# A queue of its own for the substitution's steps in a planner that orders the engines' work

## The chip, the core and the metric

The kernel runs on one core of a Trainium2 chip. Five engines work beside each other, each with a queue that it runs in order: PE (TensorE, matmuls), DVE (VectorE), ACT (ScalarE), POOL (GpSimd) and SP (SyncE, which here issues all DMAs). The metric is the device time of one execution in microseconds (us); less is better.

## What is computed

One layer of a hybrid decoder for 2,048 new tokens and 8 short sequences of 4: a gated short convolution and an RWKV-7 branch on the same normalised input, merged by gates, projected, added to the input and normalised. Cut to its core:

```python
h = _rmsnorm(x, norm_g)
p = jnp.einsum('bsd,dn->bsn', h, w_in)                 # all projections: 1024 -> 10368 columns
u = cg * xin; conv = sum(conv_w[j] * u_ext[:, j:j + s] for j in range(CONV_W))
y_c = bg * conv * jax.nn.silu(zc)
xm = p_rwkv + (prev - p_rwkv) * mu_shift               # token shift: r, k, v, z and two small ones
def step(S, inp):                                      # per head, token after token
    sa = jnp.einsum('bhvk,bhk->bhv', S, -kk_t)
    S = S * d_t[:, :, None, :] + sa[..., None] * (kk_t * a_t)[:, :, None, :] + v_t[..., None] * k_t[:, :, None, :]
    return S, jnp.einsum('bhvk,bhk->bhv', S, r_t)
yn = group_norm(ys); y_r = (yn + bonus) * jax.nn.silu(zr)
m = jax.nn.sigmoid(gc) * (y_c @ w_out_c) + jax.nn.sigmoid(gr) * (y_r @ w_out_r)
out = rmsnorm(x + m @ w_o)
```

## The kernel before

**Tiling.** The 2,048 tokens are taken in four sets (`th`, 0 to 3) of 512 columns; the last also carries the 8 sequences. The 16 heads are taken in eight pairs (`p`). One round of the main loop is one pair of one set: 32 rounds. In each round PE runs a main stream of ten projection blocks or so (`Block`), each 24 matmuls of 128x128 by 512 columns (8 pieces of K, each as high x high, low x high, high x low, in fp32r). Matmuls of the other work are put between them.

**Blocks.** A block takes its weights with `take_w`. In the first set the weights come in as f32 (`wraw`); ACT writes the high part, DVE the low part (`whl<-wraw,whl`, in `w_lows`), and both go to DRAM, from where the later sets read them ready-made. A mixed block (k, r, v, z: `mixed_block`) begins with a copy on POOL of one column of what is carried over from the set before, `tmp<-carry`; when its matmuls are done ACT writes `tmp<-ip,vec`, DVE combines it into `kT`, `rT` or `vT` (`rT<-ip,omu,tmp`, which reads the column that POOL copied too), and POOL copies the last column back, `carry<-tmp`.

**Side work.** The RWKV recurrence of a pair is worked in chunks of 64 tokens, by generators that run beside the main stream: `rwkv_keys`, `rwkv_solve`, `rwkv_merge`, `rwkv_load`, `rwkv_chain`, `rwkv_out`. `rwkv_solve` inverts triangular blocks of 32 rows, all of a pair at once, by substitution on POOL, 31 rows from 31 down to 1, with two operations for each row, every one reading what the one before wrote:

```python
for j in range(31, 0, -1):
    c0 = j // 4
    G.tensor_tensor(out=tv, in0=Mi[:, j, 0:j]..., in1=X[:, c0:8, j:j + 1]..., op=ALU.mult)
    G.tensor_tensor(out=X[:, c0:8, 0:j], in0=X[:, c0:8, 0:j], in1=tv, op=ALU.add)
    yield W["inv"]
```

These 62 operations are "the steps" in what follows (`tt<-Mi,X` and `X<-X,tt` in the profile). When they are done DVE transposes X (`Mi<-X`), ACT copies it into place (`Xbd<-Mi`, four copies), DVE transposes two parts back (`Mc<-Xbd`), and PE multiplies them (`pt<-Mc,GM` and `pt<-Mc,Mo`, 16 small matmuls), all of it in `rwkv_merge` but the first. `rwkv_out` normalises the pair's rows before: sums on DVE, `nw` on DVE, a power on POOL (`mu<-nw,mhalf`, in `rsq_steps`), further DVE work; later two products of 512 columns on POOL. POOL also does one product of 512 columns for each convolution (`cv<-cv,tmp`) and small copies and fills for `pe`.

**What sets the order.** The program is written out by a planner. Every engine call goes through `Traced`, which has a cost for it in ns (`Traced.cost`), and `Clock.add` places it in planned time: not before its operands are ready (`_hits`), and in the first gap of its engine's list of busy stretches (`Clock.gap`). `Clock.busy` has one list each for DVE, ACT and POOL. Two operations of POOL of which one needs the other are placed at least 60 ns apart. `Clock.held` keeps POOL's operations and those of DVE that read two operands from SBUF off each other: a later placed one moves behind the other. An operation that has been placed is not moved again. At the end the operations of each of the three engines are sorted by planned start and chained in that order, except for kinds of work in `LOOSE`. `Clock.kind` is the kind of side work that is being written ("solve" for `rwkv_solve`, nothing for the main stream).

PE's queue is in the order in which the program is written. `Side.run` gives a generator its turn after each matmul of the main stream when its share of the round has come (`CUTS`: "solve" from 0.30 to 0.68 of a round in the first three sets) and when what it named in its last `yield` is ready in planned time, by `clock.ready` against `clock.t["PE"]`. The steps name nothing, so that those of a row are written as soon as the share allows, ahead of the planned time at which they run. The matmuls `pt<-Mc` are written when the plan has both `Mc<-Xbd` done.

Of the kernel before, what the change touches and what calls it, by code (L numbers as in the profile page):

```python
# [54 lines left out]
OVERLAP = {"DVE": (83, 13), "ACT": (60, 18)}  # L55


class Clock:
# [3 lines left out]
    def __init__(self):  # L62
        self.t = dict.fromkeys(("PE", "DVE", "ACT", "POOL", "SP"), 0.0)
        self.log, self.home = {}, {}
        self.mode = (128, 128)
        self.busy = {"DVE": [], "ACT": [], "POOL": []}
        self.touched = {}
        self.kind = None
        self.begun, self.planning = {}, False
        self.held = {"DVE": [], "POOL": []}  # L70
# [41 lines left out]
    def gap(self, eng, start, cost):  # L112


        b = self.busy[eng]
        if len(b) >= 200:
            start = max(start, b[0][1])
        i = len(b)
        while i and b[i - 1][1] > start:
            i -= 1  # L120
        for s, e in b[i:]:
            if s >= start + cost:
                break
            start = max(start, e)
        return start
# [5 lines left out]
    def ready(self, aps):  # L131
        return max([e[4] for ap in aps for e in self._hits(ap)], default=0.0)

    def add(self, eng, outs, ins, cost, lag=60.0, dual=False):
        start = max([self.t["PE"] - PAST if eng in self.busy else self.t[eng]] + [e[4] for ap in ins for e in self._hits(ap) if e[6] != eng] +
                    [e[4] - 26.0 if eng in OVERLAP else e[5] + 60.0 * (eng == "POOL") for ap in (*ins, *outs) for e in self._hits(ap) if e[6] == eng] +
                    [self.touched.get((eng, ap.tensor.name), 0.0) for ap in (*ins, *outs)] +
                    [e[5] + 60.0 * (e[7] != eng) for ap in outs for e in self._hits(ap)])
        took = cost
        if eng in OVERLAP:  # L140
            over, drain = OVERLAP[eng]
            p0 = self.boxes(outs[0])[0][0]
            took = cost - over if p0 == 0 else cost + over + 2 * drain
        if eng in self.busy:
            start = self.gap(eng, start, took)
        if eng == "POOL" or dual:
            for s, e in self.held["POOL" if eng == "DVE" else "DVE"]:
                if s <= start < e:
                    start = self.gap(eng, e, took)
                    break  # L150
            self.held[eng] = self.held[eng][-60:] + [(start, start + cost)]
        end = start + cost
        for ap in (*ins, *outs):
            self.touched[eng, ap.tensor.name] = start
        if eng in self.busy:
            b = self.busy[eng]
            i = len(b)
            while i and b[i - 1][0] > start:
                i -= 1
            b.insert(i, (start, start + took))  # L160
            del b[:-200]
        self.t[eng] = max(self.t[eng], end)
        for ap in ins:
            for e in self._hits(ap):
                if end > e[5]:
                    e[5], e[7] = end, eng
        for ap in outs:
            for p0, p1, f0, f1 in self.boxes(ap):
                old = self.log.setdefault(self.name(ap), [])
                old[:] = [e for e in old if not (p0 <= e[0] and e[1] <= p1 and f0 <= e[2] and e[3] <= f1)][-95:]  # L170
                old.append([p0, p1, f0, f1, end + lag, end, eng, eng])
        return start
# [77 lines left out]
class Traced:  # L250
# [23 lines left out]
    def cost(self, op, out, ins, k):  # L274
        n = out.free_size()
        if self.name == "PE":
            turned = op == "transpose"
            lhs, rhs = (ins[0], ins[1]) if turned else (k["lhsT"], k["rhs"])
            part = [next(x for x in (32, 64, 128) if v <= x) for v in (lhs.ap[0][1], lhs.free_size())]
            mode = tuple(part)  # L280
            if turned:
                t, late = max(0.85 * n, 30.0), 272.0
            elif rhs.dtype == F32R:
                mode, t, late = (P, P), 8 + 0.4375 * n, 175 + 0.43 * n
            elif mode == (P, P):
                t, late = max(1.667 * n + 3, 216.0), max(382.0 if n >= P else 328.0, 175 + 1.7 * n)
            elif mode == (32, 32):
                t, late = 30.5 * max(1.0, n / 32), 212.0
            elif mode[1] == 64:
                t, late = (59.6 if mode[0] == 64 else 55.4) * max(1.0, n / 64), 300.0  # L290
            elif mode == (64, P):
                t, late = (0.93 * max(n, 64) if n <= P else 0.93 * n), 250 + 1.7 * n
            else:
                t, late = 1.667 * max(n, 32), 300.0
            if mode != self.clock.mode:
                t, late = t + 165, late + 225
                self.clock.mode = mode
            return t, late - t + SLACK
        if self.name == "DVE":
            per = {"transpose": 1.12 if n <= 256 else 1.86, "tensor_tensor_scan": 2.1, "reciprocal": 6.1}.get(op, 1.05)  # L300
            if op == "tensor_reduce":
                n = ins[0].free_size()
            if op == "tensor_scalar" and ins[0].space != PSUM:
                per = 0.587
            one = op == "scalar_tensor_tensor" and isinstance(k["scalar"], bass.AP)
            return 145 + per * n + 58 * one
        if self.name == "ACT":
            strided = n > 64 and list(ins[0].ap)[-1][0] > 1
            return (155 if ins[0].space == PSUM else 190) + (1.9 if strided else 0.84) * n + 100 * max(0, len(ins) - 1) + 0.0
        if k.get("op") == ALU.pow:  # L310
            return 1650.0
        return 218 + 2.09 * n if op == "tensor_tensor" else 120 + 1.0 * n


class Queue:
# [26 lines left out]
def hybrid_kernel(tc, x_prompt, x_sample, state_conv, state_shift, state_rwkv, norm_g, w_in, conv_w,  # L342
# [1231 lines left out]
    def comb():  # L1574

        add, sub = ALU.add, ALU.subtract
        for w, src in (("c", w_out_c[0]), ("r", w_out_r[0]), ("o", w_o[0])):
            for j in range(4):
# [9 lines left out]
                if w == "o":  # L1588
                    for q in ("11", "12", "21", "22"):
                        yield from part_of(w, q, j, qr[q], 0.5)  # L1590
                    combined("11", "12", "11", sub)
                    yield from part_of(w, "t1", j, qr["11"], 0.5)
                    combined("12", "22", "12", sub)
                    yield from part_of(w, "t3", j, qr["12"], 0.5)
                    combined("22", "22", "11", sub)
                    yield from part_of(w, "t2", j, qr["22"], 0.5)
                    combined("21", "21", "22", sub)
                    yield from part_of(w, "t4", j, qr["21"], 0.5)
                else:
                    for q in ("11", "12", "21", "22") if w == "c" else ("11", "12", "22"):  # L1600
                        yield from part_of(w, q, j, qr[q])
                    combined("22", "21", "22", add)
                    yield from part_of(w, "s1", j, qr["22"])
                    combined("21", "11", "21", sub)
                    yield from part_of(w, "s3", j, qr["21"])
                    combined("22", "22", "11", sub)
                    yield from part_of(w, "s2", j, qr["22"])
                    combined("12", "12", "22", sub)
                    yield from part_of(w, "s4", j, qr["12"])
# [259 lines left out]
    def make(n, c, parts=(0, 1)):  # L1869
# [5 lines left out]
        src, js = Y if w != "o" else M, slice(2 * c, 2 * c + 2)  # L1875
        hi, lo = (ROOMS[n % 3][:, i, js, 0:wd] for i in range(2))
        add, sub = ALU.add, ALU.subtract

        def at(q):
# [251 lines left out]
```

## Time and profile before

| | us |
|---|---|
| median of 3 runs | 3110.27 (3109.02 to 3111.27) |
| the profiled execution | 3108.97 |
| its span, first to last instruction | 3107.1 |
| PE busy | 2999.2 |
| DVE busy | 1754.3 |
| ACT busy | 1341.9 |
| POOL busy | 894.9 |

A row of the page's groups has the line, the engine and the operation, what it writes and reads, how often, its busy time and the mean of one in ns, and the idle time of the engine before it with what ended it. The steps are two of POOL's rows and 311.2 + 313.1 = 624.3 us of its 894.9:

```profile
L260 POOL TENSOR_TENSOR tt<-Mi,X 128x60 f32<-128x60 f32 (+24 forms) x992 | 311.2, 314 | 492.3 <-DVE Mi L260 378.3
L260 POOL TENSOR_TENSOR X<-X,tt 128x60 f32<-128x60 f32 (+24 forms) x992 | 313.1, 316 | 77.5
```

All engine operations have line 260, that of the helper which records them, so groups are told apart by their tiles. Busy time of PE is from matmuls that are pipelined, with modelled ends; the granted clock is the share of full speed that the throttle left PE in a stretch.

### The profile page before, as it was taken

To read this page: it belongs to the slowest core of one execution; us is meant where nothing else is said; L and a number is where in the kernel's file an instruction comes from. 1 tells how busy PE (TensorE), PEld (TensorE's weight loads), DVE (VectorE), ACT (ScalarE), POOL (GpSimd) and SP (SyncE) were. 2 spreads that over 40 slices of the span, in tenths; PEclk is the share of its full clock that TensorE was granted. 3 is DMA by queue.
4 is the path that set the end of the run, shared out by engine and by line. 5 is a ranking of instruction groups with operands and counts; after the bars stand their busy time and mean duration, and the time that the engine had idled before them with its cause. 6 is when DMAs were issued, how large, how long until landed. Compare 5 with 4: busy or idle time off the path is not lost.

```text
span 3107.1 us, 56220 instructions
## 1 busy us (share of the span) xinstructions
PE 2999.2 (97%) x21418; PEld 2576.1 (83%) x21418; DVE 1754.3 (56%) x3634; ACT 1341.9 (43%) x2691; POOL 894.9 (29%) x2492
## 2 busy tenths in 40 slices
PE   7899898999999999999999999999999999999998
PEld 6677776788888888888888889998999898888996
DVE  5465555565555555655554445455555554486575
ACT  5454454454445445444444444444444442224223
POOL 2233333333333333333333333233333330000000
PEclk9999999999999999999999999999999999999999
DMA  8776676666766676666644445443444357988775
GB/s 270 245 226 218 213 251 208 210 228 212 240 223 233 233 239 235 224 230 235 234 175 160 160 146 178 142 136 124 142 142 143 126 168 233 348 324 298 279 258 191
DMA packets 293938, 659.16 MB, mean 212 GB/s; under 512 B 46394, under 2 KB 162227, under 8 KB 242982
## 3 DMA queue, kind: packets, MB, share of 16 engines
q1 hardware_dynamic: 293670, 655.58, 62.1%
q8 instruction: 169, 2.77, 0.3%
q14 instruction: 99, 0.81, 0.1%
HBM read 472.81 MB, written 182.69 MB: 211 GB/s over the span
## 4 chain that ended last, share of the span: by engine, by line
PE 64%; POOL 9%; issue 5%; DVE 5%; ACT 2%; DMA 1%; SPq 0%; POOLq 0%; DVEq 0%; ACTq 0%
PE ip L260 39%; PE acc L260 12%; PE pt L260 8%; POOL X L260 4%; POOL tt L260 4%; PE pb L260 3%; PE pa L260 1%; DVE tmp L260 1%; ACT Xbd L260 1%; DVE Mi L260 1%; DVE sq L260 0%; ACT tmp L260 0%; DMA Y<-yr 0%; DVE cv L260 0%; POOL cv L260 0%
## 5 line engine op out<-in xcount | busy, mean ns | idle before, releaser
L260 PE MATMUL ip<-XH,whl 128*128 128x512 f32 (+3 forms) x7088 | 1948.1, 355 | 54.2 <-DVE whl L260 35.9
L260 PEld LDWEIGHTS ip<-XH,whl 128*128 128x128 f32 x7088 | 1228.5, 190 | 198.5 <-DVE whl L260 40.7
L260 PE MATMUL ip<-XL,whl 128*128 128x512 f32 (+3 forms) x3544 | 1253.8, 354 | 1.2 <-POOL XL L260 1.2
L260 PEld LDWEIGHTS ip<-XL,whl 128*128 128x128 f32 x3544 | 675.5, 191 | 75.0 <-issue 8.6
L260 POOL TENSOR_TENSOR tt<-Mi,X 128x60 f32<-128x60 f32 (+24 forms) x992 | 311.2, 314 | 492.3 <-DVE Mi L260 378.3
L260 POOL TENSOR_TENSOR X<-X,tt 128x60 f32<-128x60 f32 (+24 forms) x992 | 313.1, 316 | 77.5
L260 DVE SCALAR_TENSOR_TENSOR S<-pb,pe,sp 64x64 f32<-64x64 f32 x512 | 143.9, 281 | 187.9 <-PE pb L260 180.0
L260 ACT ACTIVATE tmp<-ip,vec 128x512 f32<-128x512 f32 (+2 forms) x174 | 103.2, 593 | 277.0 <-PE ip L260 275.2
L260 ACT ACTIVATE sp<-S,pe 128x128 f32<-128x128 f32 x256 | 102.5, 400 | 207.4 <-DVE S L260 206.0
L260 DVE TENSOR_TENSOR UB<-pa,P 64x64 f32<-64x64 f32 x512 | 110.6, 216 | 129.2 <-PE pa L260 123.2
L260 ACT COPY SV<-pb 64x128 f32<-64x128 f32 x256 | 65.8, 257 | 234.7 <-PE pb L260 233.1
L260 POOL TENSOR_TENSOR f<-f,mhalf 128x1 f32<-128x1 f32 (+1 forms) x17 | 12.5, 742 | 459.9 <-DVE f L260 458.0
L260 DVE SCALAR_TENSOR_TENSOR rT<-ip,omu,tmp 128x256 f32<-128x256 f32 (+3 forms) x59 | 28.3, 509 | 188.4 <-POOL tmp L260 179.5
L260 POOL TENSOR_TENSOR cv<-cv,tmp 128x512 f32<-128x512 f32 (+1 forms) x32 | 48.2, 1507 | 279.6 <-DVE tmp L260 279.5
L260 POOL COPY pe<-tmp 128x8 f32<-128x8 f32 x40 | 11.1, 280 | 359.5 <-ACT tmp L260 346.8
L260 DVE TENSOR_TENSOR whl<-wraw,whl 128x1024 fp32r<-128x1024 f32 x81 | 101.6, 1257 | 21.4 <-ACT whl L260 20.5
L260 ACT COPY Xbd<-Mi 32x256 f32<-32x256 f32 x128 | 87.8, 686 | 59.3 <-DVE Mi L260 57.4
L260 PEld LDWEIGHTS pb<-UB,Xbd 128*128 128x128 f32 x512 | 86.7, 188 | 29.7 <-issue 6.7
L260 ACT ACTIVATE tmp<-ip 128x512 f32<-128x512 f32 (+2 forms) x126 | 62.9, 499 | 103.4 <-PE ip L260 99.1
L260 DVE TENSOR_TENSOR GM<-pt,mask_p 128x512 f32<-128x512 f32 x128 | 82.5, 686 | 44.2 <-PE pt L260 43.6
L260 PEld LDWEIGHTS pa<-S,AR 128*128 128x128 f32 x512 | 87.4, 188 | 23.7 <-DVE S L260 11.7
L260 PEld LDWEIGHTS pb<-SV,BKt 128*128 128x128 f32 x512 | 89.1, 188 | 21.0 <-ACT SV L260 7.1
(554 smaller groups left out, 4598.8 us busy)
## 6 DMA issues: line engine op xcount, KB each, us to landing
wraw<-in_w_in_dram SPq DMA_DIRECT2D x81, 512.0 KB
whl<-w_k SPq DMA_DIRECT2D x24, 1024.0 KB
whl<-w_r SPq DMA_DIRECT2D x24, 1024.0 KB
whl<-w_v SPq DMA_DIRECT2D x24, 1024.0 KB
whl<-w_z SPq DMA_DIRECT2D x24, 1024.0 KB
whl<-w_xin SPq DMA_DIRECT2D x24, 1024.0 KB
whl<-w_cg SPq DMA_DIRECT2D x24, 1024.0 KB
whl<-w_zc SPq DMA_DIRECT2D x24, 1024.0 KB
```

The costliest lines, as they stand in the source:

```text
L260: r = f(*a, **k)
```

## The change

A fourth list, "STEPS", joins the busy lists. An operation on POOL of kind "solve" looks for a gap in STEPS first and then in POOL's list, and is entered in STEPS alone. Any other operation on POOL looks for a gap in POOL's list, which holds no steps any more, and is entered there. So the steps keep out of the way of other operations that were placed before, and other operations are placed without regard to the steps; by the sorting at the end they come between them. The distance between two dependent operations of POOL becomes 75 ns for 60, and an element-wise operation of two tensors on POOL is costed at 190 + 2.05n ns for 218 + 2.09n, with n its elements in a partition. No operation is added, removed or changed. The diff:

```diff
-        self.busy = {"DVE": [], "ACT": [], "POOL": []}
+        self.busy = {"DVE": [], "ACT": [], "POOL": [], "STEPS": []}
...
-                    [e[4] - 26.0 if eng in OVERLAP else e[5] + 60.0 * (eng == "POOL") for ap in (*ins, *outs) for e in self._hits(ap) if e[6] == eng] +
+                    [e[4] - 26.0 if eng in OVERLAP else e[5] + 75.0 * (eng == "POOL") for ap in (*ins, *outs) for e in self._hits(ap) if e[6] == eng] +
...
+        queue = "STEPS" if eng == "POOL" and self.kind == "solve" else eng
         if eng in self.busy:
-            start = self.gap(eng, start, took)
+            start = self.gap(queue, start, took)
+            if queue == "STEPS":
+                start = self.gap(eng, start, took)
         if eng == "POOL" or dual:
             for s, e in self.held["POOL" if eng == "DVE" else "DVE"]:
                 if s <= start < e:
-                    start = self.gap(eng, e, took)
+                    start = self.gap(queue, e, took)
                     break
...
         if eng in self.busy:
-            b = self.busy[eng]
+            b = self.busy[queue]
...
-        return 218 + 2.09 * n if op == "tensor_tensor" else 120 + 1.0 * n
+        return 190 + 2.05 * n if op == "tensor_tensor" else 120 + 1.0 * n
```

## The prediction

> **What bounds the kernel now.** I read the busy shares of the page first, then the waits of PE, then those of DVE, and last the timeline around the longest waits.
>
> ```profile
> span 3107.1 us, 56220 instructions
> PE 2999.2 (97%) x21418; PEld 2576.1 (83%) x21418; DVE 1754.3 (56%) x3634; ACT 1341.9 (43%) x2691; POOL 894.9 (29%) x2492
> ```
>
> PE is the bound. No matmul is added or taken away, so the time can change only in PE's idle time and in its clock. PE's waits (who <- for whom: us in total, times, longest):
>
> ```profile
> PE ip L260 <- DVE whl L260: 35.9, 9, 11.3
> PE pt L260 <- DVE Mc L260: 12.9, 9, 4.3
> PE ip L260 <- DVE rT L260: 11.1, 4, 4.8
> PE ip L260 <- DVE vT L260: 4.7, 1, 4.7
> ```
>
> The reader is to see two kinds. In `whl`, `rT` and `vT`, 51.7 us together, PE waits for DVE in the projections. In `Mc`, 12.9 us, it waits for the result of the substitution, `rwkv_solve`. DVE's own waits name what holds DVE in the first kind:
>
> ```profile
> DVE rT L260 <- POOL tmp L260: 179.5, 27, 15.7
> ```
>
> 27 times DVE stands still because one small copy on POOL, `tmp<-carry` (the first column of a mixed block), is late. Why it is late stands in the timeline of one such place, DVE first, then POOL, then PE (start us, us, engine, line, operation, [idle before <- releaser]):
>
> ```profile
> 262.42 0.17 DVE L260 TENSOR_SCALAR nw<-mu__2816 128x8 f32<-128x8 f32 x1
> 274.04 0.75 DVE L260 SCALAR_TENSOR_TENSOR rT<-ip,omu,tmp 128x512 f32<-128x512 f32 x1 [11.45 <-POOL tmp L260]
> 274.71 0.43 DVE L260 STREAM_TRANSPOSE Mi<-X 128x256 f32<-128x256 f32 x1
> 275.07 1.18 DVE L260 TENSOR_TENSOR whl<-wraw,whl 128x1024 fp32r<-128x1024 f32 x1
> ```
>
> ```profile
> 273.56 0.21 POOL L260 TENSOR_TENSOR X<-X,tt 128x8 f32<-128x8 f32 x1
> 273.70 0.19 POOL L260 COPY carry<-tmp 128x1 f32<-128x1 f32 x1
> 273.82 0.18 POOL L260 COPY tmp<-carry 128x1 f32<-128x1 f32 x1
> 273.96 1.64 POOL L260 TENSOR_TENSOR mu__2816<-nw,mhalf 128x8 f32<-128x8 f32 x1
> ```
>
> ```profile
> 269.27 0.63 PE L260 MATMUL ip<-XH,whl 128*128 128x512 f32 x2
> 269.74 0.40 PE L260 MATMUL ip<-XL,whl 128*128 128x512 f32 x1
> 269.97 0.39 PE L260 MATMUL ip<-XH,whl 128*128 128x512 f32 x1
> 276.30 0.80 PE L260 MATMUL ip<-XH,whl 128*128 128x512 f32 x1 [5.94 <-DVE whl L260]
> ```
>
> The 62 steps of a substitution have filled POOL; the copies and the power `mu<-nw,mhalf` come right behind the last step, at 273.56, though the power's operand was there at 262.59. DVE sits at `rT`, the split of the next weights (`whl`) sits behind `rT`, and PE is idle for 5.94 us. In the plan of before the steps are 60 ns apart, no other operation fits between two, and so each takes its place after the last step placed so far.
>
> **What goes away.** Eight such places hold nearly all of the first kind. Here they are as stretches, each from PE's stop to the end of the slow clock behind it (the start and end of the stretch, us, then busy us of PE, PEld, DVE, ACT and POOL, the granted clock, DMA):
>
> ```profile
> 109.49:124.72 15.23, 3.94 (x10) 3.14 (x10) 3.68 (x4) 0.50 (x1) 7.88 (x33) 0.66 0.22 67
> 270.36:281.73 11.37, 5.43 (x14) 4.27 (x14) 6.02 (x12) 4.08 (x6) 5.51 (x18) 0.70 0.41 135
> 353.91:363.65 9.74, 2.95 (x7) 2.37 (x8) 5.02 (x10) 4.05 (x6) 6.18 (x21) 0.65 0.25 82
> 437.03:445.57 8.54, 2.98 (x8) 2.40 (x8) 4.00 (x5) 1.43 (x2) 4.95 (x18) 0.80 0.15 38
> 533.93:544.55 10.62, 3.81 (x9) 2.75 (x9) 6.12 (x13) 4.78 (x7) 4.92 (x18) 0.68 0.23 77
> 611.44:619.65 8.21, 4.28 (x12) 3.19 (x12) 6.19 (x13) 5.08 (x8) 4.33 (x13) 0.79 0.40 121
> 2135.67:2145.40 9.73, 4.96 (x21) 4.94 (x21) 1.66 (x6) 1.61 (x5) 7.59 (x26) 0.65 0.10 40
> 2459.67:2466.26 6.59, 3.26 (x13) 3.24 (x14) 1.60 (x5) 0.48 (x1) 5.34 (x20) 0.74 0.14 60
> sum 80.03, PE 31.61 PEld 26.31 DVE 34.30 ACT 22.01 POOL 46.70; mean PE 3.95 PEld 3.29 DVE 4.29 ACT 2.75 POOL 5.84
> ```
>
> In 80.03 us PE issues 94 matmuls. Undisturbed, three take 0.70 us (269.27 to 269.97 above), 0.233 each: 60 in the first six stretches make 14.0 us, and 34 in the last two, of about half that width, 4.0 us. So **80.0 - 18.0 = 62 us** go if no such stall is left. Its cover: with the copy between the steps, `rT` runs when its matmul is done, and the split is ready before PE asks.
>
> **What is moved, and its price on the chip.** The others now go between the steps. The copies cost nothing, as one that happened to fall there already shows:
>
> ```profile
> 916.55 0.32 POOL L260 TENSOR_TENSOR X<-X,tt 128x65 f32<-128x65 f32 x1
> 916.81 0.19 POOL L260 COPY tmp<-carry 128x1 f32<-128x1 f32 x1
> 916.95 0.30 POOL L260 TENSOR_TENSOR tt<-Mi,X 128x60 f32<-128x60 f32 x1
> ```
>
> Without it the step would start some 0.08 to 0.09 us after 916.87, which is where it starts. The copy lies in the pause in which a step waits for the one before. The power is too long for that pause: 1.64 - 0.09 = **1.55 us** by which the last step, and so X, comes later on the chip. The plan doesn't see this: all steps of the pair have been placed when the power is placed (in before it stands behind the last of them), and a placed step isn't moved. Queued behind the power on POOL are the remaining steps; for the last of them wait the transposition `Mi<-X` on DVE, the copies `Xbd<-Mi` on ACT, the transpositions `Mc<-Xbd` on DVE, and the matmuls `pt<-Mc` on PE. No DMA is issued from POOL here, and SP's queue keeps its order.
>
> **What the new costs do.** Steps are costed at 190 + 2.05n for 218 + 2.09n, and 75 ns apart for 60. The sizes n of a substitution's 62 operations, (8 - j//4)j twice for j = 31 to 1, add to 3,120. The plan's chain shrinks by 62 x (28 - 15) + 0.04 x 3,120 ns = **0.93 us**. PE's queue is written in the plan's order, with `pt<-Mc` where the plan holds X for finished. So PE comes to `pt<-Mc` 0.93 us earlier, while X comes 1.55 us later: 2.48 us against PE. That `rT` no longer stands before `Mi<-X` is known to the plan as well, so both sides gain the same from it.
>
> How much margin is there? Two pairs, one near each end: DVE's second `Mc`, and the first matmul of PE that waits for it or finds it ready.
>
> ```profile
> 929.62 0.43 DVE L260 STREAM_TRANSPOSE Mc<-Xbd 32x256 f32<-32x256 f32 x1 [0.16 <-ACT Xbd L260]
> 1670.58 0.44 DVE L260 STREAM_TRANSPOSE Mc<-Xbd 32x256 f32<-32x256 f32 x1 [0.56 <-ACT Xbd L260]
> ```
>
> ```profile
> 930.11 0.21 PE L260 MATMUL pt<-Mc,Mo 32*32 32x32 f32 x1 [0.38 <-DVE Mc L260]
> 1672.89 0.21 PE L260 MATMUL pt<-Mc,GM 32*32 32x32 f32 x1
> ```
>
> In the first the margin is -0.38 us (PE waits), in the second 1672.89 - 1671.02 = 1.87. I take the middle, 0.75, so a stall of 1.73 us in each of the 27 pairs in which DVE waited (27 in its row above): **46.7 us**. With a margin of 1.87 everywhere it would be 16, with -0.38 77. The other five pairs have no power in their steps and lose at most 0.93 each, **4.6 us**.
>
> Then the clock. Stretches with short stalls at `Mc`, same columns as above:
>
> ```profile
> 996.00:1006.00 10.00, 8.89 (x98) 6.76 (x96) 4.57 (x11) 7.70 (x15) 3.72 (x11) 1.00 0.77 270
> 1889.38:1896.23 6.85, 4.43 (x48) 4.24 (x48) 3.95 (x10) 6.24 (x12) 0.37 (x1) 0.75 0.39 146
> ```
>
> 1.11 us of idle time left the clock at 1.00; 6.85 - 4.43 = 2.42 us brought 0.75 over 6.85 us, 1.7 us lost. A stall of 1.73 lies between the two, so I count half of the 27: 13.5 x 1.7 = **23 us**, with none and all of them (46) as bounds.
>
> The Trainium skill, "TensorE: Matmul & The Clock Gate", section "Why this matters for your kernels", asks for no PE gaps above some 3 us, since one idle window brings back the half clock. By that rule stalls of 1.73 us would cost no clock; the stretch at 1889 speaks against it.
>
> **The sum**, from the profiled execution's 3108.97 us (its span and 1.9 us around it): 3108.97 - 62.0 + 46.7 + 4.6 + 23 = 3121.3. The median of the runs is 1.3 above the profiled one, so **3122 us**. The gain is on DVE's wait, and what is late next is X itself.
>
> **The rivals.**
>
> 1. *The margin holds.* If X isn't late on the chip by the power (because the plan puts `pt<-Mc` behind something else that is late enough), only 0.93 - 0.75 = 0.18 us x 27 = 5 us return: 3108.97 - 62 + 5, with the 1.3 some **3053 us**, faster. For it: 1.87 of margin at 1672.89. Against it: nine waits for `Mc` already, 12.9 us, with the power behind the steps. The point where it decides: with s the mean new stall, 27 x (s + 0.85) + 4.6 = 62 at s = 1.3 us. Below that the change gains.
> 2. *Short stalls leave the clock alone.* As the forecast, without the 23 us: **3099 us**. For it the row at 996, against it that at 1889.
> 3. *DVE slows the steps.* DVE, no longer held, does its work beside the steps:
>
> ```profile
> 260.44 1.35 DVE L260 TENSOR_TENSOR whl<-wraw,whl 128x1024 fp32r<-128x1024 f32 x1
> 260.78 1.17 POOL L260 TENSOR_TENSOR tt<-Mi,X 128x68 f32<-128x68 f32 x1
> ```
>
> A step of 68 elements took 1.17 us beside a split, against 0.32 for 65 elements above. One or two more of those per substitution, 0.85 each and unseen by the plan, make the stall about 2.7 us, 73 us for the 27, and all of them then halve the clock, 46 us: 3108.97 - 62 + 73 + 4.6 + 46, about **3171 us**. Against it: outside the first quarter few splits are left. The Trainium skill, "SBUF — State Buffer", section "Who interferes with whom", says that a DVE instruction with two SBUF inputs and a GpSimd one that reads SBUF exclude each other; the row agrees.
> 4. *It doesn't do what it says*: the others stay behind the steps, or PE's stalls only change place: **3110 us**. Against it: the power's operand is there 11 us before it runs.
>
> **How the numbers follow.** Forecast 0.35 (own range 3103 to 3148), rival 1 0.25, rival 2 0.17, rival 3 0.12, rival 4 0.11. The range, 3050 to 3152, leaves out about 0.08 below, for a full gain without any return, and 0.12 above. Within 0.2% (3104 to 3116.5; a measurement of this kernel tells about that much from no change) lie 0.06 of the forecast, 0.03 of rival 2 and 0.06 of rival 4: 0.15. Faster: rival 1, 0.13 of rival 2 and 0.02 of rival 4: 0.40. Slower: 0.29 of the forecast, 0.01 of rival 2, rival 3 and 0.03 of rival 4: 0.45.
>
> **What would show it.** DVE's wait for POOL `tmp` falls from 179.5 us to under 30; PE's for `whl`, `rT` and `vT` from 51.7 to under 8. The power stands among the steps, with X's last step 1 to 2 us further from the first. PE's wait for `Mc` rises from 12.9 to 40 to 80 us, with more short stretches at half clock. If the wait for `Mc` stays under 25 us, the step with the margin is wrong and the kernel is faster; if DVE still waits for POOL, the first step is.

## The result and the profile after

| | before | after |
|---|---|---|
| median of 12 runs, us | 3110.62 (3107.74 to 3114.31) | 3120.95 (3110.93 to 3131.42) |
| ratio, 95% interval | | 1.0032 (1.0019 to 1.0045) |
| profiled span, us | 3107.1 | 3123.8 |
| PE busy, us | 2999.2 | 3026.6 |
| span less PE busy, us | 107.9 | 97.2 |
| mean granted clock | 0.989 | 0.982 |

The change costs 0.3%. The profiled execution after took 3125.49 us, 4.5 us more than the median, so that its rows are those of one of the longer runs. Of the twelve runs of the last kernel in the table of experiments two took 8418 and 8569 us at full clock, why isn't known, and its figures leave them out. The last three rows hold the surprise: PE is idle for 10.7 us less than before, and the kernel is slower, because PE is busy for 27.4 us more with the same 21,418 matmuls. The page after:

```profile
span 3123.8 us, 56082 instructions
PE 3026.6 (97%) x21418; PEld 2604.2 (83%) x21418; DVE 1770.9 (57%) x3634; ACT 1341.2 (43%) x2691; POOL 905.6 (29%) x2492
```

Where PE is idle has changed altogether. The groups of PE in the kernel after, then the same groups before (xcount | busy, mean ns of one | idle time before them, and what ended it):

```profile
L263 PE MATMUL ip<-XH,whl 128*128 128x512 f32 (+3 forms) x7088 | 1961.9, 356 | 7.7 <-DVE whl L263 7.2 <-DVE tmp L263 0.2
L263 PE MATMUL pt<-Mc,GM 32*32 32x32 f32 x512 | 28.6, 202 | 28.6 <-DVE Mc L263 16.0 <-DVE u L263 6.0 <-DVE Yc L263 4.2
L263 PE MATMUL pt<-Mc,Mo 32*32 32x32 f32 x512 | 24.7, 203 | 18.4 <-DVE Mc L263 18.3
```

```profile
L260 PE MATMUL ip<-XH,whl 128*128 128x512 f32 (+3 forms) x7088 | 1948.1, 355 | 54.2 <-DVE whl L260 35.9 <-DVE rT L260 11.1 <-DVE vT L260 4.7
L260 PE MATMUL pt<-Mc,GM 32*32 32x32 f32 x512 | 24.5, 195 | 7.3 <-DVE Mc L260 7.3
L260 PE MATMUL pt<-Mc,Mo 32*32 32x32 f32 x512 | 22.7, 195 | 5.6 <-DVE Mc L260 5.6
```

Before the projections PE was idle for 54.2 us and is now for 7.7. Before `pt<-Mc` it was idle for 7.3 + 5.6 = 12.9 and is now for 28.6 + 18.4 = 47.0. Of these 47.0 us 34.2 are put down to `Mc`, and two stalls of 6.0 us together, put down to `u`, end 0.15 us behind the end of an `Mc`; most of the remaining 6.8 us ends with `Yc` or with an operation on ACT. DVE no longer waits for the copies, and waits for X instead:

```profile
DVE Mi L263 <- POOL X L263: 81.9, 26, 6.6
```

Before, that row read 19.3 us, and `rT` waited 179.5 for POOL's `tmp`, a row that is gone.

One pair shows the whole of it. POOL's timeline after (start us, us):

```profile
890.09 0.24 POOL L263 TENSOR_TENSOR tt<-Mi,X 128x31 f32<-128x31 f32 x1 [10.62 <-DVE Mi L263]
...
913.02 0.24 POOL L263 TENSOR_TENSOR X<-X,tt 128x28 f32<-128x28 f32 x1
913.23 1.65 POOL L263 TENSOR_TENSOR mu__9342<-nw,mhalf 128x8 f32<-128x8 f32 x1
914.84 0.23 POOL L263 TENSOR_TENSOR tt<-Mi,X 128x24 f32<-128x24 f32 x1
...
916.38 0.65 POOL L263 TENSOR_TENSOR X<-X,tt 128x8 f32<-128x8 f32 x1
```

The power stands between two steps: the next starts at 914.84, where 913.26 + 0.08, the usual pause, would be 913.34. That is 1.50 us. From the first step's start to the last one's end it is 917.03 - 890.09 = 26.94 us. The same pair before:

```profile
900.67 0.59 POOL L260 TENSOR_TENSOR tt<-Mi,X 128x31 f32<-128x31 f32 x1 [15.20 <-DVE Mi L260]
...
925.78 0.21 POOL L260 TENSOR_TENSOR X<-X,tt 128x8 f32<-128x8 f32 x1
```

925.99 - 900.67 = 25.32 us, 1.62 less. PE, after, stands still for that pair twice, for 0.77 us at 917.97 and for 1.10 before the second `Mc`:

```profile
917.34 0.63 PE L263 MATMUL ip<-XH,whl 128*128 128x512 f32 x2
918.74 0.24 PE L263 MATMUL pt<-Mc,GM 32*32 32x32 f32 x2 [0.77 <-DVE Mc L263]
```

And the clock falls to half behind it. Behind a stall of nearly the same size in another pair, the second row, it doesn't (start and end of the stretch, us, then busy us of PE, PEld, DVE, ACT and POOL, the granted clock, DMA):

```profile
917.97:930.21 12.24, 10.37 (x86) 8.15 (x85) 4.12 (x6) 7.21 (x14) 2.86 (x4) 0.58 0.51 175
1071.83:1083.83 12.00, 10.18 (x130) 8.17 (x130) 2.41 (x5) 8.29 (x17) 3.06 (x5) 1.00 0.61 187
```

Both stretches have 1.8 to 1.9 us of idle time. In the first PE gets 86 matmuls done in 12.2 us, in the second 130. The idle time is the small part of the cost in the first of these pairs.

### The profile page after: what moved, and what is told of

Same layout as the page of the kernel before. It is cut to its first block, busy times and chain, and to the rows that moved or that the text cites. A ratio compares the mean times of both kernels' runs of the same rounds, so it can differ in the third digit from the quotient of the medians.

```text
span 3123.8 us, 56082 instructions
## 1 busy us (share of the span) xinstructions
PE 3026.6 (97%) x21418; PEld 2604.2 (83%) x21418; DVE 1770.9 (57%) x3634; ACT 1341.2 (43%) x2691; POOL 905.6 (29%) x2492
## 4 chain that ended last, share of the span: by engine, by line
PE 57%; POOL 19%; issue 11%; DVE 8%; ACT 3%; DMA 2%; SPq 0%; POOLq 0%; DVEq 0%; ACTq 0%
PE ip L263 33%; PE acc L263 12%; POOL X L263 8%; POOL tt L263 8%; PE pt L263 8%; PE pb L263 2%; DVE tmp L263 2%; ACT Xbd L263 2%; PE pa L263 1%; DVE Mi L263 1%; POOL cv L263 1%; DVE whl L263 1%; ACT tmp L263 1%; DMA gc<-tmp 1%; DVE cv L263 1%
## 5 line engine op out<-in xcount | busy, mean ns | idle before, releaser
L263 PEld LDWEIGHTS ip<-XL,whl 128*128 128x128 f32 x3544 | 681.1, 192 | 71.7 <-issue 4.1
L263 POOL TENSOR_TENSOR tt<-Mi,X 128x60 f32<-128x60 f32 (+24 forms) x992 | 318.0, 321 | 487.2 <-DVE Mi L263 400.3
L263 POOL TENSOR_TENSOR X<-X,tt 128x60 f32<-128x60 f32 (+24 forms) x992 | 321.5, 324 | 71.4
L263 PE MATMUL pb<-UB,Xbd 128*128 128x128 f32 x512 | 103.3, 284 | 4.5 <-DVE UB L263 3.8
L263 PE MATMUL pa<-S,AR 128*128 128x128 f32 x512 | 101.4, 280 | 5.8 <-DVE S L263 5.7
```

The costliest lines, as they stand in the source:

```text
L263: r = f(*a, **k)
```

## The experiments

My theory: the gain is real (DVE is free, PE's stalls in the projections are gone) and is given back because PE's queue has `pt<-Mc` earlier than X is there, by the power among the steps and by a planned chain that has become 0.93 us shorter; short stalls then halve the clock. The rivals: DVE's work beside the steps slows them; or PE's place for `pt<-Mc` isn't what costs. In the table "idle at `Mc`" is PE's idle time before the matmuls `pt<-Mc`, and "at half clock" the time in which the trace's record of the clock shows half, without the last stretch behind the final matmuls; both, and the mean clock, are those of the profiled execution. Each ratio is to the kernel before, run on the same chip.

| kernel | median, us | ratio to before, 95% | idle at `Mc` | at half clock | mean clock |
|---|---|---|---|---|---|
| before | | 1 | 12.9 | 64.9 | 0.989 |
| after | 3120.95 | 1.0032 (1.0019 to 1.0045) | 47.0 | 109.2 | 0.982 |
| queue alone, old costs | 3108.21 | 0.9987 (0.9978 to 0.9997) | 33.8 | 85.3 | 0.985 |
| new costs alone, old queue | 3117.77 | 1.0018 (1.0009 to 1.0026) | 16.8 | 81.9 | 0.986 |
| after, power behind the steps | 3078.33 | 0.9893 (0.9878 to 0.9908) | 21.8 | 44.4 | 0.992 |
| after, steps planned 115 ns apart | 3108.72 | 0.9990 (0.9980 to 1.0000) | 37.6 | 88.7 | 0.985 |
| after, X counted 1.25 us later | 3094.91 | 0.9949 (0.9936 to 0.9963) | 32.9 | 71.7 | 0.988 |
| after, X counted 2.5 us later | 3068.14 | 0.9865 (0.9852 to 0.9877) | 18.0 | 44.4 | 0.992 |
| after, X counted 3.75 us later | 3068.33 | 0.9868 (0.9852 to 0.9885) | 8.0 | 34.1 | 0.993 |
| after, X counted 5.0 us later | 3067.72 | 0.9857 (0.9842 to 0.9872) | 6.8 | 30.7 | 0.994 |
| power behind, X counted 1.0 us later | 3083.41 | 0.9917 (0.9904 to 0.9929) | 13.0 | 51.2 | 0.991 |
| before, X counted 1.0 us later | 3106.82 | 0.9983 (0.9975 to 0.9992) | 2.9 | 78.5 | 0.986 |

**The two halves of the change, each alone.** The queue with the old costs:

```diff
-... e[5] + 75.0 * (eng == "POOL") ...
+... e[5] + 60.0 * (eng == "POOL") ...
-        return 190 + 2.05 * n if op == "tensor_tensor" else 120 + 1.0 * n
+        return 218 + 2.09 * n if op == "tensor_tensor" else 120 + 1.0 * n
```

> The queue of its own, with the old costs (218 + 2.09n, 60 ns). Theory (PE comes to pt<-Mc before X is there, partly by the power between the steps, partly by the plan's chain that shrank by 0.93 us): the plan's X is 0.93 us later than in the changed kernel, so PE's idle time before pt<-Mc falls from 47 us to about 20 to 30, half clock from 109 us to 60 to 85, time 3085 to 3105. DVE's wait for POOL tmp stays under 15 us. Rival (the steps are slowed by DVE's work beside them, by several us, or the gain was never there): 3115 to 3130, idle before pt<-Mc above 40 us.

And the new costs in the kernel before, the same lines the other way round:

> The new costs (190 + 2.05n, 75 ns) in the kernel before, one list for POOL. Theory: DVE's wait for POOL tmp stays near 180 to 200 us and the stalls of the first kind stay; PE comes 0.93 us earlier to pt<-Mc, its idle time there goes from 13 us to 20 to 35; time 3115 to 3135, slower than before. Rival (the shrunk chain is harmless, the return comes from the power alone): 3105 to 3115.

The queue alone is 0.13% faster than before, and the shrunk costs take it from there to 0.32% slower. By themselves, in the kernel before, they cost 0.18%. Both go the theory's way, and both less far than it said: the queue alone still has 33.8 us of idle time at `Mc` where 20 to 30 were expected, and its time, 3108.21, is above the range given; with the new costs alone the idle time is 16.8 us where 20 to 35 were expected. A planned chain that is 0.93 us longer doesn't make up for a power of 1.5 us.

**The power put behind the steps again.**

```diff
-        queue = "STEPS" if eng == "POOL" and self.kind == "solve" else eng
+        queue = "STEPS" if eng == "POOL" and (self.kind == "solve" or cost == 1650.0) else eng
```

> The changed kernel, but the power (cost 1650) is placed in the steps' list too, so behind the steps as before; the copies stay between them. Theory: X comes 1.55 us earlier on the chip than in the changed kernel, idle time before pt<-Mc from 47 to under 20 us, half clock under 70 us, DVE's wait for POOL tmp under 15 us: 3050 to 3085, faster than both. Rival (X is late because of DVE's work beside the steps, the power is nothing): idle before pt<-Mc stays above 35 us, 3110 to 3125.

3078.33 us, 1.1% faster than before and in the range given, and the stalls in the projections stay away; the idle time at `Mc`, 21.8 us, is just above the 20 expected. Its groups of PE:

```profile
L263 PE MATMUL ip<-XH,whl 128*128 128x512 f32 (+3 forms) x7088 | 1942.6, 354 | 6.1 <-DVE whl L263 5.4 <-ACT whl L263 0.4 <-DVE tmp L263 0.2
L263 PE MATMUL pt<-Mc,GM 32*32 32x32 f32 x512 | 25.8, 197 | 11.3 <-DVE Mc L263 6.9 <-DVE Yc L263 2.5 <-DVE u L263 1.4
L263 PE MATMUL pt<-Mc,Mo 32*32 32x32 f32 x512 | 23.1, 197 | 10.5 <-DVE Mc L263 10.5
```

So with the copies alone among the steps the gain stays, and with the power among them too, in the changed kernel's plan, it is given back. This run is no clean test of the rival that DVE's work beside the steps is what makes X late, since its steps, 628.0 us in all, are faster than the changed kernel's as well. How much longer the steps have become there shows in their two groups on POOL (x992 each: busy us, mean ns):

```profile
L263 POOL TENSOR_TENSOR tt<-Mi,X 128x60 f32<-128x60 f32 (+24 forms) x992 | 318.0, 321 | 487.2 <-DVE Mi L263 400.3
L263 POOL TENSOR_TENSOR X<-X,tt 128x60 f32<-128x60 f32 (+24 forms) x992 | 321.5, 324 | 71.4
```

318.0 + 321.5 = 639.5 us in all, against 624.3 in the kernel before: 15.2 us, or 0.5 us for each of the 32 substitutions. It is there, at a third of the power's price. Worked out from all 32 substitutions, the time from the first step to the end of the last grew by 2.14 us, from 24.42 to 26.56: 1.3 by the power, 0.5 by the slower steps, 0.4 by copies and products of 512 columns among the steps.

**The plan alone, first way: steps further apart.**

```diff
-... e[5] + 75.0 * (eng == "POOL") ...
+... e[5] + (115.0 if self.kind == "solve" else 75.0) * (eng == "POOL") ...
```

> The changed kernel, with the steps planned 115 ns apart for 75: the plan's X comes 62 x 40 ns = 2.48 us later, on the chip nothing is longer. Theory: PE comes to pt<-Mc when X is there; idle time before it from 47 us to under 10, half clock under 45 us, 3045 to 3070. Rival (the stalls at pt<-Mc are not a matter of where PE's queue has it; X's end itself holds the main stream by other ways): 3105 to 3125, the idle time moves to other matmuls.

3108.72 us: better than the changed kernel, far from what the theory said. The mean time from a substitution's first step to the end of its last is 27.79 us here. Where the plan stretches the steps, more of what comes later falls among them, and the chip, whose steps aren't stretched, has to run it there. So in this kernel:

```profile
601.88 0.23 POOL L263 TENSOR_TENSOR X<-X,tt 128x24 f32<-128x24 f32 x1
602.07 1.28 POOL L263 TENSOR_TENSOR tmp<-tmp,bv 128x512 f32<-128x512 f32 x1
603.31 0.21 POOL L263 TENSOR_TENSOR tt<-Mi,X 128x16 f32<-128x16 f32 x1
```

```profile
1436.25 0.18 POOL L263 COPY carry<-tmp 128x1 f32<-128x1 f32 x1 [0.58 <-ACT tmp L263]
```

A product of 512 columns has come between two steps (12 of `rwkv_out`'s products are among steps here, 4 in the changed kernel), and elsewhere POOL stands for 0.58 us at a copy whose operand isn't there yet, with steps behind it. The idle time before such operations among the steps is 0.76 us for each substitution, worked out from all 32, against 0.11 in the changed kernel. The margin in the plan was 2.48 us, and the chip took back 27.79 - 26.56 = 1.23. This edit was no clean test. What is left of the margin, 1.25 us, also brought less than the same 1.25 us in the next test; why is open.

**The plan alone, second way: only X's end.** Steps and others keep their places; the plan counts X as readable later.

```diff
-        took = cost
+        took, lag, self.late = cost, lag + self.late, 0.0
...
+            clock.late = 1250.0 if j == 1 else 0.0
             G.tensor_tensor(out=X[:, c0:8, 0:j], in0=X[:, c0:8, 0:j], in1=tv, op=ALU.add)
```

> The changed kernel; the plan counts X as finished 1.25 us after its last step, and nothing else differs (steps stay 75 ns apart in the plan, so others aren't moved among them). Theory (PE's place for pt<-Mc against X is what costs): idle time before pt<-Mc from 47 us to 15 to 25, half clock from 109 us to 50 to 75, 3070 to 3095. If a step's distance of 115 ns failed because X itself came later by it, this works where that didn't. Rival (PE's place isn't it): 3110 to 3125 and idle time of PE about as in the changed kernel, 97 us.

> The same with 2.5 us. Theory: idle time before pt<-Mc under 12 us, half clock under 50 us, 3050 to 3075. Rival: as in the run with 1.25 us, or slower, if what follows X now comes too late for the next round.

> As with 2.5 us, with 3.75. Each 1.25 us brought 26 to 27 us so far (3121, 3095, 3068), and 18 us of idle time before pt<-Mc are left at 2.5, most of it waits of 1.09 us for the second Mc. Theory: these go, idle before pt<-Mc under 9 us, half clock under 35 us, 3050 to 3062. Rival (at 2.5 us the margin covers X, and more only makes what follows late): 3064 to 3080, idle time in ip, pa and pb grows.

> As above, with 5.0 us: where the return ends. Theory: nothing is left to win at pt<-Mc, within 8 us of the run with 3.75. Rival: the rounds no longer hold the work, idle time before pa and pb rises over 15 us, slower than with 3.75 by 10 us and more.

3121, 3095, 3068, 3068, 3068 us: 26 and 27 us for the first two steps of 1.25, then nothing. No operation on the chip is shorter here, and POOL's order differs only where the rest of the plan moved with it. The times with 1.25 and 2.5 are in the ranges that were written down, though the idle time at `Mc` fell less than expected (32.9 us for 15 to 25, 18.0 for under 12). With 3.75 the idle time and the half clock are as expected, and the time is above its range, in that of the rival; with 5.0 it is within the 8 us expected. With 2.5 us the power is still among the steps, and the kernel is 1.35% faster than before. These are its two groups at `Mc` on PE and the steps on POOL:

```profile
L263 PE MATMUL pt<-Mc,GM 32*32 32x32 f32 x512 | 24.9, 196 | 6.6 <-DVE Mc L263 3.6 <-DVE u L263 3.0
L263 PE MATMUL pt<-Mc,Mo 32*32 32x32 f32 x512 | 22.9, 196 | 11.4 <-DVE Mc L263 11.3
L263 POOL TENSOR_TENSOR X<-X,tt 128x60 f32<-128x60 f32 (+24 forms) x992 | 324.1, 327 | 72.0
L263 POOL TENSOR_TENSOR tt<-Mi,X 128x60 f32<-128x60 f32 (+24 forms) x992 | 318.4, 321 | 487.5 <-DVE Mi L263 374.6 <-PE ip L263 23.9 <-DVE S L263 18.7
```

The steps take 324.1 + 318.4 = 642.5 us, no less than in the changed kernel, and the power is where it was: X is as late on the chip, and only what reads it has another place in the plan. The margin moves the place of DVE's `Mi<-X` as well as that of `pt<-Mc`; the runs don't part the two. Two of its pairs, with the same stall of 1.09 us for the second `Mc`:

```profile
895.85:903.14 7.29, 6.20 (x67) 4.82 (x69) 2.91 (x3) 5.37 (x10) 2.87 (x4) 0.77 0.65 223
971.59:978.88 7.29, 6.20 (x84) 4.94 (x83) 2.89 (x3) 6.12 (x12) 2.87 (x4) 1.00 0.68 226
```

7.29 - 6.20 is the same 1.09 us of idle time in both; in one the clock halves and 67 matmuls get done, in the other 84. With 3.75 us the idle time at `Mc` falls to 8 us, but PE waits longer elsewhere, 7.9 us for 4.0 for DVE's `Yc` before the transpositions of the pair before and 5.6 for 1.7 for `S` before `pa`. Its idle time as a whole falls by 4 us only, and its busy time not at all, though the half clock is 10 us less; why is open.

**Both remedies together, and the margin without the queue.**

> The power behind the steps, and X counted as finished 1.0 us after its last step. Theory: of the 21.8 us before pt<-Mc that were left with the power behind, under 10 remain; half clock under 40 us; 3050 to 3070, the fastest. Rival (what is left comes from elsewhere): 3073 to 3083 as with the power behind alone.

> The kernel before, with X counted as finished 1.0 us after its last step. It shows what a margin is worth without the new queue. Theory: the 13 us before pt<-Mc fall to under 6 with their share of the half clock, and the stalls of the first kind stay: 3093 to 3107. Rival (the margin, not the queue, is what the faster kernels live on): 3050 to 3085.

The first did not do what I expected. With the power behind the steps a margin of 1.0 us lowers the idle time at `Mc` from 21.8 to 13.0 and the kernel is slower, 3083 for 3078. Its trace has PE standing 5.6 us for `whl` and 3.6 and 3.8 us elsewhere in the first set, with DVE at `Mi<-X` for 4 to 5 us each time; why that set came out worse than without the margin stays open. In the kernel before, the margin takes the idle time at `Mc` from 12.9 to 2.9, as expected, and the time falls by 0.17%, at the upper end of the range given. The half clock did not fall with the idle time (78.5 us for 64.9), and the stalls before the projections remain, 56.8 us for 54.2. That settles the rival that the margin alone is what the faster kernels live on: it is worth 0.17% without the queue, and 1.7% with it (3120.95 to 3068.14).

## Why the prediction was right

3122 us were forecast and 3120.95 measured, on the side that was given. The mechanism was the one forecast; the sum came out better than its terms.

- **What bounds the kernel** was read rightly: PE's idle time before the projections came from DVE at `rT`, and DVE's from the copy behind the steps. The forecast said that DVE's wait for `tmp` falls under 30 us and PE's for `whl`, `rT` and `vT` under 8; the one left the list of DVE's longest waits and the other is 7.2.
- **What goes away**: 62 us, of which 80.03 - 31.61 = 48.4 idle and 13.6 slow clock. Measured, the idle time before the projections fell by 54.2 - 7.7 = 46.5. The slow clock behind these stalls can't be told from the rest in the trace after.
- **The power** was sized at 1.55 us and takes 1.50 where it was looked at; it stands among the steps in 28 of 32 substitutions, 27 were assumed. That X is late by the power alone was not right: its last step is 2.14 us further from the first, just past the 1 to 2 us given as a sign, and the rest comes from the slower steps and from copies and products that were put at nothing.
- **The stall at `Mc`.** 46.7 + 4.6 us were added to the time, and 47.0 - 12.9 = 34.1 came. Most of the miss is in the sum: a stall worked out from a margin is the whole stall of a pair, and the 12.9 us that the kernel before has already were not taken off. As a whole, 51.3 were forecast and 47.0 came. In the trace after 25 of the 32 pairs stall, 1.88 us on the mean, where 27 at 1.73 were assumed. That the middle between two pairs came so near was luck: no row gave it, the stalls lie between 0.15 and 4.6 us, and X was later than assumed.
- **The clock** was sized too small. The forecast gave 23 us to it, half of the stalls at 1.7 each. PE is busy for 27.4 us more although, by the forecast's own figure, the 13.6 of the first kind are gone: 41 us. The half came out: by the record of the clock, with 15 of the 25 stalls a stretch at half clock begins during the stall or within 4 us behind it. The step that failed is the price. These 15 stretches are 88.7 us in all, 5.9 each or about 3.0 us lost, where the one row at 1889 gave 1.7. That row was misread as well: of its 2.42 us of idle time only 0.70 + 1.02 = 1.72 stand before `pt<-Mc`, so that a stall of just the size forecast had halved the clock in the kernel before.

The last two misses are -17 and +18 us and cancel. That the total is within 2 us is luck; that the return would be about as large as the gain, so that the change ends near no gain, was worked out. Rival 1 (the margin holds, 3053) comes near to what the margin of 2.5 us makes of the kernel: 3068. Rival 2 (short stalls leave the clock alone) is refuted by the stall of 1.87 us above, with a clock of 0.58 behind it. Rival 3 (DVE slows the steps) is real at 0.5 us for each substitution, a quarter of X's delay. Rival 4 (the others stay behind the steps) is out: the power is among them, and `rT` no longer waits.

## What to carry to other kernels

A plan that lets small operations into a chain of dependent ones must tell the chain's readers what they cost: here a small copy alone between two steps was free, the one operation of 1.6 us was not, and what it broke was the place in the plan of what reads X, down to the matmuls in PE's queue, which had been fixed without it. Where a queue is in order and its places come from a plan, test the plan's error directly, by counting one result later and changing nothing else; the time then shows where the error ends. And look at PE's busy time beside its idle time: the idle time fell here while the kernel got slower.

## What the runs showed of the hardware

Stalls far shorter than I thought halve PE's clock, and the same stall does it in one pair and not in the next: 1.09 us twice, with clocks of 0.77 and 1.00 over the next 7.3 us. The Trainium skill, "TensorE: Matmul & The Clock Gate", section "Why this matters for your kernels", asks for no gaps above some 3 us; the rows here differ from it. Its section "What's actually happening" says that activity is counted in a free-running window of 3.4 us, and the record agrees: its stretches at half clock are one to four times 3.41 us long, and in each of the twelve traces all of their starts and ends lie on one grid of 3.413 us, within 0.002 us over the 3 ms (the end of the trace aside). So it matters how a stall lies to the grid. These are the windows on it with the stall of 1.87 us and with that of 1.82 (columns as above):

```profile
916.56:919.97 3.41, 1.65 (x9) 0.93 (x7) 2.80 (x6) 2.37 (x4) 0.70 (x3) 1.00 0.44 175
1070.15:1073.56 3.41, 1.92 (x10) 1.16 (x8) 2.20 (x5) 2.17 (x4) 0.88 (x3) 1.00 0.20 76
```

Nearly the whole of the first stall falls into one window, with 1.65 us of PE's time busy, and the clock is halved from its end on; the second is shared with the next window. Where the border is stays open: over the twelve traces, windows in which PE is busy for 0.45 to 0.7 of the time stand before both. It would also explain the wider spread of the changed kernel's runs, 3110.93 to 3131.42, against 3107.74 to 3114.31 before: the run of 3110.93 has a mean clock of 0.987, that of 3131.42 one of 0.980. That isn't tested.

A copy of one column between two dependent steps on POOL costs them next to nothing, though it takes 0.18 us. Worked out from the trace after, the pause from one step's end to the next one's start is 78 ns at the median without a copy (1,813 cases) and 80 with one (92); by the profile the copy overlaps the steps on both sides. Two copies in a row make it 0.2 us (14 cases), and a copy whose operand isn't there yet holds the steps behind it.
